# Lo parts of 17 mLSTM weight tiles on VectorE, and the order of loads, sums and splits in three later stages

## The chip, the cores and the metric

One core of a Trainium2 chip runs the kernel in one launch. The metric is device time in microseconds (us), the median of several runs. In the profile PE is TensorE, DVE VectorE, ACT ScalarE, POOL GpSimd and SP SyncE, which here only issues DMAs.

## The reference, cut to what matters

One layer of a diffusion backbone over 1024 latent tokens with 256 context tokens as a prefix, width 1024, all in float32.

```python
def layer(x, c, ctx, c_ctx):
    h = modulate(x, ...)                 # adaLN-modulated RMSNorm, also of ctx
    k, v, ig, fg, q, o, cu, cb, cc, gates = split(h @ w_in)
    conv = ...                           # width-3 convolution along grid rows, gated
    hs = mlstm_chunked(q, k, v, ig, log_sigmoid(fg), state of ctx)   # 8 heads, 2 directions
    merged = sigmoid(gates_a) * (conv @ w_a) + sigmoid(gates_b) * (norm(hs) * sigmoid(o) @ w_b)
    x = x + gate1 * (merged @ w_out)
    h2 = modulate(x, ...)
    return x + gate2 * (square(relu(h2 @ w_f1)) @ w_f2)              # width 4096
```

The output is this latent stream after a last RMSNorm, 1024 x 1024.

## The kernel before, in words

All matrices are multiplied in three passes: a float32 operand is split into `hi`, its value rounded to fp32r, and `lo`, the rest, also in fp32r, and the product is hi·hi + hi·lo + lo·hi (`PASS`). The helper `split` (line 127) makes both parts: `hi` by a copy on ScalarE, `lo` by a subtraction on the engine that its argument `eng_lo` names, or on GpSimd where none is given. Nearly every instruction of the profile carries line 75, the line of a small wrapper that calls the engine; operations are told apart by the names of their tiles. Loads are issued on SP (line 94, `dma`), stores on POOL (line 91, `store`).

The work goes through these stages (us of the span): adaLN and norms to about 100; the mLSTM with its projections to about 517; Strassen products of weight pairs ("H pairs") to about 900; two further GEMMs in 56 steps (`gsteps`) to 1053; the output projection to 1160; Strassen pairs of the MLP's first matrix ("F pairs") to 1450; the MLP's second matrix to 1772.

**Weight tiles.** In the mLSTM stage and in the output projection, tiles of 128 x 1024 are taken from a list, `stream`, of (source, engine of the lo part). `fetch(n)` (line 144) loads and splits tiles until `n` stand ready, `take()` takes one; their pool `ws` has two buffers for each of `wst`, `whi`, `wlo`. For each head pair 1 to 3 the list (line 349) has two V tiles, a K and a Q tile; then come eight O tiles (line 350). Only the second V tile names VectorE. While a tile's matmuls run, a generator `mlstm` (line 572) is pumped for pieces of the mLSTM chunks: on VectorE `e` (decay exponents), `cs` (states), `sdt` (scores times decay), `dn` and `rcp` (the denominator) and `hs` (the output); on GpSimd `wqz` (weighted q); on TensorE `psm`, `pso`, `psu`. The order of these pieces on each engine is found by a scheduler from the dependencies and from the time that it holds each instruction to take; stages with `pinned[0]` set, the H pairs, `gsteps` and F pairs among them, keep the order in which they are written.

**Pairs.** The class `Pairs` (line 831) multiplies two rows of weights, `a` and `c`, by seven products `m1` to `m7` instead of eight. `steady(p0)` (line 942) runs a pair's products while it prepares the next pair's factors: `first_row` splits `a`, `second_block` a half of `c`, `sums` (line 870) makes four sums in place on VectorE, `sums_row` splits them into `sh` (ScalarE) and `sl` (VectorE), and `load_pair` loads the rows of the pair after it. `early` is the first pair that runs in this steady form: 1 for the H pairs, 3 for the F pairs. In that pair `sums` comes after `m5`, in later ones after `m2`. `load_row` (line 845) issues its load unpinned, so that the scheduler places it among SP's other loads.

**MLP pairs.** `f11`, `f22`, `f12`, `f21` finish the four results of a pair, in tiles `fc` and `fd` (in the profile `Ffc` and `Ffd` from the home buffers), with relu and square on ScalarE. `fpost` (line 1467) sums them for the second matrix's own Strassen form and stores them to `fq` in DRAM; its two results `Ff12` and `Ff34` have one home page each, but for pair 1, which takes two pages `f` of the pool `pg` (37 pages).

**The output projection.** Its eight `w_o` tiles (line 1305) have VectorE as lo engine. `fetch(1)` at the third-last of the `gsteps` (line 1328) loads and splits the first one; the others follow as `take` is called. In the same stretch VectorE finishes the merge (`gate`, `u4` and `Ml`, the lo part of the merged operand).

Of the kernel before, what the change touches and what calls it, by code (L numbers as in the profile page):

```python
# [13 lines left out]
P = 128  # L14
# [5 lines left out]
H = 8  # L20
# [19 lines left out]
U_K, U_Q, U_O, U_X, U_GC, U_GB, U_MA, U_MB = 0, 4, 8, 16, 24, 32, 40, 48  # L40
# [20 lines left out]
def tile_block(ctx: ExitStack, tc: tile.TileContext, x, cx, w_mod1, w_mod, w_v0, w_v, w_unit, w_conv, w_mls, w_o, w_f1, w_f2, cols_d, rows_d, cst_d, out):  # L61
    nc = tc.nc
    pinned = [False]
# [18 lines left out]
    V, A, G, PE, SY = Engine(nc.vector), Engine(nc.scalar), Engine(nc.gpsimd), Engine(nc.tensor), nc.sync  # L82
# [10 lines left out]
    def dma(dst, src, pin=True):  # L93
        i = SY.dma_start(dst, src)
        if pin:
            tc.keep_in_program_order(i)
# [3 lines left out]
    def nm(s):  # L100
        uid[0] += 1
        return f"{s}_{uid[0]}"

    def page(shape, dt=F32, name="pg"):
        return pg.tile(shape, dt, tag="pg", name=nm(name))
# [27 lines left out]
    def load_w_now(src, eng_lo=None, eng_hi=None):  # L133
        n = 1024
        st = ws.tile([P, n], F32, tag="wst", name=nm("wst"))
        dma(st, src, pin=False)
        hi = ws.tile([P, n], F32R, tag="whi", name=nm("whi"))
        lo = ws.tile([P, n], F32R, tag="wlo", name=nm("wlo"))
        split(st, hi, lo, eng_hi, eng_lo)
        return hi, lo  # L140

    stream, ready = [], []

    def fetch(n=1):
        while stream and len(ready) < n:
            ready.append(load_w_now(*stream.pop(0)))
# [26 lines left out]
    def keep(f):  # L173


        def call(*a, **kw):
            p, pinned[0] = pinned[0], True
            f(*a, **kw)
            pinned[0] = p

        return call
# [164 lines left out]


    for p in range(1, 4):
        stream += [(w_v[p - 1, :, 0:1024],), (w_v[p - 1, :, 1024:2048], V), (w_unit[U_K + p],), (w_unit[U_Q + p],)]
    stream += [(w_unit[U_O + h],) for h in range(H)] + [(w_unit[U_MB + 4 * i],) for i in range(2)]  # L350


    gb = wm.tile([P, 32], F32, name="gb", bufs=1)
# [449 lines left out]
    def home(n_, i, n, make, dt=F32, shape=(P, 1024)):  # L803

        if (n_, i % n) not in homes:
            homes[n_, i % n] = make(list(shape), dt, n_)
        return homes[n_, i % n]

    def leave(pre):

        for k in [k for k in homes if k[0].startswith(pre)]:
            del homes[k]

    def in_ws(shape, dt, name):
        return ws.tile(shape, dt, tag=name, name=nm(name))
# [7 lines left out]
    def add(o, a, b):  # L823
        V.tensor_tensor(o, a, b, op=ALU.add)
# [6 lines left out]
    class Pairs:  # L831
# [13 lines left out]
        def load_row(self, p, i, own=False):  # L845
            if p >= self.early:
                st = self.home("wst" if p % 2 else "wst2", i, 2, (lambda s_, d_, n_: in_ws(s_, d_, "wst")) if p % 2 else page)
            else:
                st = page([P, 1024], name="wst") if own else in_ws([P, 1024], F32, "wst")
            dma(st, self.rows(p)[i], pin=False)  # L850
            self.raw.setdefault(p, []).append(st)

        def load_pair(self, p):
# [88 lines left out]
        def steady(self, p0, last=None, each=lambda p: None):  # L942
            for p in range(p0, self.n):
                n = p + 1 if p + 1 < self.n else None
                if p > self.early:
                    self.end_d(p - 1)
                self.m1(p)
                if p == self.early:
                    self.end_d(p - 1)
                self.post(p - 1)  # L950
                self.m6(p)
                each(p)
                if n:
                    self.first_row(n)
                    self.second_block(n)
                    if n + 1 < self.n:
                        self.load_pair(n + 1)
                self.m2(p)
                if n and p > self.early:
                    self.sums(n)  # L960
                if n is None and last:
                    last()
                self.m7(p)
                each(p)
                self.m5(p)
                if p == self.early:
                    self.sums(n)
                if n:
                    self.sums_row(n, 0)
                self.m3(p)  # L970
                each(p)
                if n:
                    self.sums_row(n, 1)
                self.m4(p)
# [244 lines left out]
    def each(p):  # L1219
        if p > HE and HPAIRS[p][0] != U_GB:  # L1220
            pump_one()
        if p == len(HPAIRS) - 2:
            drain()
# [6 lines left out]
    gsteps = [(g, m, k) for g in range(2) for m in ORDER7 for k in range(4)]  # L1230
# [32 lines left out]
    def g_prepare(i):  # L1263
        hi, lo = ring("whi", i, F32R), ring("wlo", i, F32R)
        for src, s in zip(gst.pop(i), (L, R)):
            split(src, hi[:, s], lo[:, s], eng_lo=V)
        gmade[i] = hi, lo
# [33 lines left out]
    def block(n_, j, pool=page):  # L1301
        return home(n_, j // 2, 2, pool, F32, (P, 2, 512))[:, j % 2, :]
# [4 lines left out]
    for i, (g, m, k) in enumerate(gsteps):  # L1307
        if i + AHEAD + 1 < len(gsteps):
            g_gather(i + AHEAD + 1)
        if i + AHEAD < len(gsteps):  # L1310
            g_prepare(i + AHEAD)
        X = sets[(g + ORDER7.index(m)) % 2]
        ab = gmade.pop(i)
        for j in range(4):
            for n_, (a, b) in enumerate(PASS):
                keep(PE.matmul)(X[j], ab[a][:, j * P : (j + 1) * P], ab[b][:, R], start=m not in (2, 4) and k == 0 and n_ == 0, stop=k == 3 and n_ == 2, skip_group_check=True)
        if m == 1:
            for n in range(2 * k, 2 * k + 2):
                gate[g, n] = page([P, D], name="gate")
                dma(gate[g, n], sgd[gemms[g][2]][n])  # L1320
                if g == 0:
                    t2[n] = gate[g, n]
        for _ in range(-(-len(later) // (4 - k))):
            later.pop(0)()
        if i == 16:
            hpost(len(HPAIRS) - 1)
            leave("H")
        if i == len(gsteps) - 3:
            fetch(1)
        if k < 3:  # L1330
            continue
        U2, V22 = [[block(n_, j, page2) for j in range(4)] for n_ in ("Gu2", "Gv")]
        for j in range(4):
            if m == 1:
                A.copy(U2[j], X[j])
            elif m == 6:
                later.append(lambda j=j, X=X: add(U2[j], X[j], U2[j]))
            elif m == 2:
                later += gated(g, j, L, lambda j=j, X=X, g=g: mul(gate[g, j][:, L], X[j], gate[g, j][:, L]))
            elif m == 7:  # L1340
                later.append(lambda j=j, X=X: add(V22[j], X[j], U2[j]))
            elif m == 5:
                U4 = [half("u4") for _ in range(4)] if j == 0 else U4
                later.append(lambda j=j, X=X, U4=U4: add(U4[j], X[j], U2[j]))
                later.append(lambda j=j, X=X: add(V22[j], X[j], V22[j]))
            elif m == 4:
                later.append(lambda j=j, X=X: add(U2[j], X[j], U2[j]))
            elif m == 3:
                later.append(lambda j=j, X=X, U4=U4: add(U4[j], X[j], U4[j]))
        if m == 2 and g:  # L1350
            later += [lambda n=n: joined(0, n) for n in range(4)]
        if m == 5:
            for j in range(4):
                later += gated(g, 4 + j, R, lambda j=j, g=g: mul(gate[g, 4 + j][:, R], V22[j], gate[g, 4 + j][:, R]))
        elif m == 4:
            for j in range(4):
                later += gated(g, 4 + j, L, lambda j=j, g=g: mul(gate[g, 4 + j][:, L], U2[j], gate[g, 4 + j][:, L]))
            if g:
                later += [lambda n=n: joined(0, n) for n in range(4, KT)]
        elif m == 3:  # L1360
            for j in range(4):
                later += gated(g, j, R, lambda j=j, g=g, U4=U4: mul(gate[g, j][:, R], U4[j], gate[g, j][:, R]))
# [103 lines left out]

    def fpost(p):
        c, d = fc.pop(p), fd.pop(p)
        g_, h_ = (home("Ff12", 0, 1, page), home("Ff34", 0, 1, in_mst)) if p != 1 else [page([P, 1024], name="f") for _ in range(2)]
        add(g_[:, L], c[:, R], d[:, R])  # L1470
        sub(g_[:, R], g_[:, L], c[:, L])
        store(fq[2][p], g_)
        sub(h_[:, L], c[:, L], c[:, R])
        sub(h_[:, R], d[:, L], g_[:, R])
        store(fq[3][p], h_)
# [267 lines left out]
    for j in range(4):  # L1743
        t = 4 + j
        cuts = (0, 512) if j < 3 else (0, CUT, 512)
        n = len(cuts)
# [118 lines left out]
```

## Time and profile before

| | |
|---|---|
| median of 3 runs | 1806.89 us (1806.43 to 1807.1) |
| the profiled execution: its time, its span | 1808.16 us, 1806.3 us |
| granted TensorE clock, mean | 0.989 |
| busy: PE, PEld | 1749.0 us (97%), 1443.5 us (80%) |
| busy: DVE, ACT, POOL | 1266.3 us (70%), 753.3 us (42%), 230.6 us (13%) |
| on the chain that ended last: PE, DVE, ACT | 69%, 3%, 2% |

The busy share is an average over stages; what bounds one of them is seen in its own stretch. Engines read and write in the order of their queues, so an instruction that waits holds up all that stand behind it on the same engine. In a timeline row the bracket at the end is the time that the engine stood idle before it and what ended that. [...]

### The profile page before, as it was taken

How to read it: one execution, taken by the hardware profiler on the slowest of the kernel's cores; microseconds unless marked ns; L12 is line 12 of the kernel's file. 1: busy time of each engine (PE TensorE's matmuls, PEld its weight loads, DVE VectorE, ACT ScalarE, POOL GpSimd, SP SyncE). 2: the span in 40 equal slices, each digit the busy share in tenths (PEclk: the TensorE clock that was granted, in tenths of full speed). 3: DMA queues.
4: the chain of work that ended last, by engine and by line, in shares of the span. 5: the costliest groups of instructions: out<-in, count | busy, mean ns of one | idle time of the engine just before them, and what ended most of it. 6: DMA issues, size and time to landing. Idle time of an engine off the chain costs nothing.

```text
span 1806.3 us, 23536 instructions
## 1 busy us (share of the span) xinstructions
PE 1749.0 (97%) x8633; PEld 1443.5 (80%) x8633; DVE 1266.3 (70%) x2207; ACT 753.3 (42%) x1237; POOL 230.6 (13%) x286
## 2 busy tenths in 40 slices
PE   6999999999999999999999999999999999999994
PEld 3898889877877888888888878877888888888884
DVE  5557564546685768879789996876666656577785
ACT  5633534456333331222244434644434444344334
POOL 3213222234320000000000001101101100000001
PEclk9999999999999999999999999999999999999997
DMA  8213141412424453534458255225434376666352
GB/s 321 76 51 84 46 91 34 85 53 77 174 95 173 164 175 99 164 122 135 172 183 297 88 187 187 82 96 190 163 129 153 143 256 195 231 224 204 104 186 93
DMA packets 102107, 261.10 MB, mean 145 GB/s; under 512 B 11624, under 2 KB 24808, under 8 KB 101992
## 3 DMA queue, kind: packets, MB, share of 16 engines
q1 hardware_dynamic: 85672, 200.88, 35.0%
q0 software_dynamic: 16320, 58.73, 8.2%
q8 instruction: 67, 1.10, 0.3%
q14 instruction: 48, 0.39, 0.1%
HBM read 198.62 MB, written 60.95 MB: 144 GB/s over the span
## 4 chain that ended last, share of the span: by engine, by line
PE 69%; DVE 3%; ACT 2%; issue 1%; DMA 0%; POOL 0%; ACTq 0%; DVEq 0%; POOLq 0%
PE psg L75 69%; ACT y L75 1%; DVE gate L75 0%; DMA fq<-Ffd 0%; ACT Fsh L75 0%; DVE wlo L75 0%; DVE y L75 0%; ACT fc L75 0%; DVE wst L75 0%; DVE fc L75 0%; DVE x L75 0%; DVE ftmp L75 0%; DVE Ff L75 0%; DVE Fsl L75 0%; DVE ol L75 0%
## 5 line engine op out<-in xcount | busy, mean ns | idle before, releaser
L75 ACT ACTIVATE whi<-wst 128x512 fp32r<-128x512 f32 (+1 forms) x238 | 195.9, 826 | 262.9 <-PE psg L75 164.8
L75 DVE TENSOR_TENSOR wlo<-wst,whi 128x512 fp32r<-128x512 f32 (+1 forms) x219 | 202.3, 927 | 123.4 <-ACT whi L75 121.6
L75 PE MATMUL psg<-whi,wlo 128*128 128x512 f32 (+2 forms) x688 | 266.5, 387 | 0.0
L75 PE MATMUL psg<-whi 128*128 128x512 f32 (+2 forms) x688 | 266.5, 387 | 0.0
L75 PE MATMUL psg<-wlo,whi 128*128 128x512 f32 (+2 forms) x688 | 266.1, 387 | 0.1
L75 PE MATMUL psg<-hh,whi 128*128 128x512 f32 x440 | 177.5, 409 | 0.7 <-ACT u L75 0.7
L75 PE MATMUL psg<-hh,wlo 128*128 128x512 f32 x440 | 173.5, 400 | 1.3 <-DVE wlo L75 1.3
L75 PE MATMUL psg<-hl,whi 128*128 128x512 f32 x440 | 173.0, 399 | 0.0
L75 PEld LDWEIGHTS psg<-wlo,whi 128*128 128x128 f32 x688 | 129.5, 188 | 27.8 <-DVE wlo L75 0.6
L75 PEld LDWEIGHTS psg<-whi,wlo 128*128 128x128 f32 x688 | 129.3, 188 | 27.2
L75 PEld LDWEIGHTS psg<-whi 128*128 128x128 f32 x688 | 129.4, 188 | 26.8
L75 PEld LDWEIGHTS psg<-hh,wlo 128*128 128x128 f32 x440 | 83.9, 191 | 20.7 <-DVE wlo L75 1.7
L75 PEld LDWEIGHTS psg<-hh,whi 128*128 128x128 f32 x440 | 83.3, 191 | 19.7 <-ACT u L75 1.1
L75 PEld LDWEIGHTS psg<-hl,whi 128*128 128x128 f32 x440 | 84.0, 191 | 17.6
L75 PE MATMUL psg<-oh,Fsl 128*128 128x512 f32 x240 | 94.9, 396 | 0.1
L75 PE MATMUL psg<-oh,Fsh 128*128 128x512 f32 x240 | 94.9, 396 | 0.0
L75 PE MATMUL psg<-ol,Fsh 128*128 128x512 f32 x240 | 94.6, 394 | 0.0
L75 DVE TENSOR_TENSOR u<-psg,u 128x512 f32<-128x512 f32 x67 | 45.8, 686 | 50.2 <-PE psg L75 48.5
L75 PE MATMUL psg<-whi,hh 128*128 128x256 f32 (+1 forms) x256 | 76.2, 297 | 0.0
L75 PE MATMUL psg<-whi,hl 128*128 128x256 f32 (+1 forms) x256 | 73.3, 286 | 0.0
L75 PE MATMUL psg<-wlo,hh 128*128 128x256 f32 (+1 forms) x256 | 73.2, 286 | 0.0
L75 POOL TENSOR_TENSOR wqz<-w,q 64x256 f32<-64x256 f32 x64 | 46.9, 735 | 140.4 <-PE pso L75 125.6
(352 smaller groups left out, 3936.6 us busy)
## 6 DMA issues: line engine op xcount, KB each, us to landing
wst<-fq SPq DMA_DIRECT2D x112, 256.0 KB, 2.8
wst<-in_w_unit_dram SPq DMA_DIRECT2D x38, 512.0 KB, 3.8
mst<-in_w_mod_dram SPq DMA_DIRECT2D x32, 512.0 KB, 4.1
wst<-in_w_f_dram SPq DMA_DIRECT2D x64, 256.0 KB, 3.0
fq<-Ff POOLq DMA_DIRECT2D x30, 512.0 KB, 3.1
wst<-in_w_f_dram SPq DMA_DIRECT2D x21, 512.0 KB, 3.5
Hwst<-in_w_unit_dram SPq DMA_DIRECT2D x18, 512.0 KB, 3.5
x<-in_x_dram SPq DMA_DIRECT2D x16, 512.0 KB, 4.7
```

Source lines behind the costliest of these rows:

```text
L75: i = f(*a, **kw)
```

## The change

Five edits. (1) The 15 entries of `stream` without an engine among the V, K, Q and O tiles get `V`, VectorE, as engine of the lo part; with three V tiles, three K, three Q and eight O tiles these are 17. (2) `load_row` pins its load where the code around it is pinned, so that the H and F pairs' loads go out in the order in which they are written. (3) In the first steady pair `sums` comes after `m2`, as in the others. (4) The last three `gsteps` fetch one `w_o` tile each, instead of the third-last alone. (5) Pair 1 of the MLP uses the home pages for its two results instead of two pages of its own.

```diff
     for p in range(1, 4):
-        stream += [(w_v[p - 1, :, 0:1024],), (w_v[p - 1, :, 1024:2048], V), (w_unit[U_K + p],), (w_unit[U_Q + p],)]
-    stream += [(w_unit[U_O + h],) for h in range(H)] + [(w_unit[U_MB + 4 * i],) for i in range(2)]
+        stream += [(w_v[p - 1, :, 0:1024], V), (w_v[p - 1, :, 1024:2048], V), (w_unit[U_K + p], V), (w_unit[U_Q + p], V)]
+    stream += [(w_unit[U_O + h], V) for h in range(H)] + [(w_unit[U_MB + 4 * i],) for i in range(2)]
...
-            dma(st, self.rows(p)[i], pin=False)
+            dma(st, self.rows(p)[i], pin=pinned[0])
...
                 self.m2(p)
-                if n and p > self.early:
+                if n:
                     self.sums(n)
...
                 self.m5(p)
-                if p == self.early:
-                    self.sums(n)
...
-        if i == len(gsteps) - 3:
-            fetch(1)
+        if i >= len(gsteps) - 3:
+            fetch(i - len(gsteps) + 4)
...
-        g_, h_ = (home("Ff12", 0, 1, page), home("Ff34", 0, 1, in_mst)) if p != 1 else [page([P, 1024], name="f") for _ in range(2)]
+        g_, h_ = home("Ff12", 0, 1, page), home("Ff34", 0, 1, in_mst)
```

What this does to the order of instructions is seen in three places, all on VectorE. The first is the mLSTM stage at head pair 2's K and Q tiles. Before (`hs_2498` is the output that TensorE waited for at 251 us):

```order
L75 TENSOR_TENSOR sdt_2748<-psm_519_2746,e_2680 128x256
L75 TENSOR_TENSOR sdt_2752<-psm_521_2750,e_2680 128x256
L75 SCALAR_TENSOR_TENSOR e_2754<-e_2754,gt_a,cst_67 128x128 x4
L75 SCALAR_TENSOR_TENSOR dn_2775<-pso_2741,dn_2775 128x2
L75 TENSOR_TENSOR va_2194<-psg_2723,vb_2191 128x2x128
L75 RECIPROCAL rcp_2778<-dn_2775 128x2
L75 SCALAR_TENSOR_TENSOR hs_2498<-pso_2741,rcp_2778,hs_2498 128x128
```

The same place with the change:

```order
L75 TENSOR_TENSOR sdt_2752<-psm_521_2750,e_2680 128x256
L75 SCALAR_TENSOR_TENSOR e_2754<-e_2754,gt_a,cst_67 128x128 x4
L75 SCALAR_TENSOR_TENSOR dn_2766<-pso_2736,dn_2766 128x2
L75 TENSOR_TENSOR dn_2775<-pso_2741,gt_gd 128x2
L75 RECIPROCAL rcp_2769<-dn_2766 128x2
L75 TENSOR_TENSOR va_2194<-psg_2723,vb_2191 128x2x128
L75 SCALAR_TENSOR_TENSOR dn_2775<-pso_2741,dn_2775 128x2
L75 TENSOR_TENSOR wlo_2800<-wst_2797,whi_2799 128x1024
L75 SCALAR_TENSOR_TENSOR hs_2497<-pso_2736,rcp_2769,hs_2497 128x128
L75 RECIPROCAL rcp_2778<-dn_2775 128x2
L75 TENSOR_TENSOR sdt_2824<-psm_539_2822,e_2754 128x256
L75 SCALAR_TENSOR_TENSOR hs_2498<-pso_2741,rcp_2778,hs_2498 128x128
```

The Q tile's lo part now stands between the `e` group and `hs_2498`, the K tile's one row ahead of the first `sdt`, and the operations of the other direction (`dn_2766`, `rcp_2769`, `hs_2497`), which stood ahead of the `e` group, stand behind it.

The second place is the output projection: `wlo_8956` before, and `wlo_8903` with the change, is the lo part of its third weight tile. Before:

```order
L75 TENSOR_TENSOR u_1159_8727<-psg_5423,u_1159_8727 128x512
L75 TENSOR_TENSOR gate_8324<-u_1156_8724,gate_8324 128x512
L75 TENSOR_TENSOR gate_8326<-u_1157_8725,gate_8326 128x512
L75 TENSOR_TENSOR gate_7751<-gate_7751,gate_8324 128x512
L75 TENSOR_TENSOR gate_7753<-gate_7753,gate_8326 128x512
L75 TENSOR_TENSOR gate_8350<-u_1158_8726,gate_8350 128x512
L75 TENSOR_TENSOR gate_8352<-u_1159_8727,gate_8352 128x512
L75 TENSOR_TENSOR gate_7776<-gate_7776,gate_8350 128x512
L75 TENSOR_TENSOR gate_7778<-gate_7778,gate_8352 128x512
L75 TENSOR_TENSOR wlo_8956<-wst_8953,whi_8955 128x1024
```

With the change:

```order
L75 TENSOR_TENSOR wlo_8873<-wst_8870,whi_8872 128x1024
L75 TENSOR_TENSOR Ml_8889<-gate_7800,Mh_8888 128x512
L75 TENSOR_TENSOR Ml_8889<-gate_7802,Mh_8888 128x512
L75 TENSOR_TENSOR Ml_8895<-gate_7824,Mh_8894 128x512
L75 TENSOR_TENSOR Ml_8895<-gate_7826,Mh_8894 128x512
L75 TENSOR_TENSOR wlo_8903<-wst_8900,whi_8902 128x1024
L75 TENSOR_TENSOR gate_8324<-u_1156_8724,gate_8324 128x512
L75 TENSOR_TENSOR gate_8326<-u_1157_8725,gate_8326 128x512
```

The third tile's lo part has moved from behind the eight `gate` operations to ahead of them; the second tile's, `wlo_8873`, now stands right ahead of the four `Ml`.

The third place is the first steady pair of the MLP, pair 3 (`Fwst` are pair 4's rows, whose sums are made in place). Before:

```order
L75 TENSOR_TENSOR Fa_1346_9966<-Fwst_1357_10131,Fa_1346_9966 128x512
L75 TENSOR_TENSOR Ffc_10204<-psg_5426,u_1358_10159 128x512
L75 TENSOR_TENSOR Ffd_10091<-psg_5425,Ffc_10204 128x512
L75 TENSOR_TENSOR Fwst_1356_10129<-Fwst_1356_10129,Fwst_1357_10131 128x512
L75 TENSOR_TENSOR Fwst_1357_10131<-Fwst_1357_10131 128x512
L75 TENSOR_TENSOR Fwst_1357_10131<-Fwst_1357_10131,Fwst_1356_10129 128x512
L75 TENSOR_TENSOR Fwst_1356_10129<-Fwst_1356_10129,Fwst_1357_10131 128x512
L75 TENSOR_TENSOR Fsl_9404<-Fwst_1357_10131,Fsh_9403 128x1024
```

With the change:

```order
L75 TENSOR_TENSOR Fa_1346_9966<-Fwst_1355_10129,Fa_1346_9966 128x512
L75 TENSOR_TENSOR Fwst_1354_10127<-Fwst_1354_10127,Fwst_1355_10129 128x512
L75 TENSOR_TENSOR Fwst_1355_10129<-Fwst_1355_10129 128x512
L75 TENSOR_TENSOR Fwst_1355_10129<-Fwst_1355_10129,Fwst_1354_10127 128x512
L75 TENSOR_TENSOR Fwst_1354_10127<-Fwst_1354_10127,Fwst_1355_10129 128x512
L75 TENSOR_TENSOR Ffc_10202<-psg_5426,u_1356_10157 128x512
L75 TENSOR_TENSOR Ffd_10091<-psg_5425,Ffc_10202 128x512
L75 TENSOR_TENSOR Fsl_9404<-Fwst_1355_10129,Fsh_9403 128x1024
```

The four sums have moved ahead of `Ffc` and `Ffd`. On SP, pair 4's two rows now go into pages that `fc` of pair 0 and `fd` had, and each pair's two rows are issued one after the other, `a` first.

## Rows read from the trace of the kernel before

**Rows 1.** The page, busy time by engine: us, share, instructions.
```profile
PE 1749.0 (97%) x8633; PEld 1443.5 (80%) x8633; DVE 1266.3 (70%) x2207; ACT 753.3 (42%) x1237; POOL 230.6 (13%) x286
```

**Rows 2.** TensorE's waits: us in total, times, longest.
```profile
PE pso L75 <- DVE hs L75: 7.2, 6, 2.6
PE psg L75 <- ACT u L75: 5.5, 3, 3.7
```

**Rows 3.** TensorE's timeline, rows with a wait: start, us, instruction, [idle before].
```profile
251.31 0.80 PE L75 MATMUL pso<-va,sdt 128*128 128x129 f32 x2 [2.57 <-DVE hs L75]
...
338.07 0.49 PE L75 MATMUL pso<-va,sdt 128*128 128x129 f32 x2 [2.62 <-DVE hs L75]
...
400.51 0.63 PE L75 MATMUL pso<-va,sdt 128*128 128x129 f32 x2 [2.11 <-DVE sdt L75]
...
565.83 0.51 PE L75 MATMUL psg<-hh,whi 128*128 128x512 f32 x1 [0.66 <-ACT u L75]
...
1068.76 0.50 PE L75 MATMUL psg<-wlo,Mh 128*128 128x512 f32 x1 [1.66 <-DVE wlo L75]
...
1243.45 0.50 PE L75 MATMUL psg<-oh,whi 128*128 128x512 f32 x1 [3.69 <-ACT u L75]
```

**Rows 4.** VectorE's timeline, 238 to 250 us.
```profile
239.86 1.13 DVE L75 SCALAR_TENSOR_TENSOR e<-e,gt_a,cst 128x128 f32<-128x128 f32 x4
...
245.12 4.83 DVE L75 SCALAR_TENSOR_TENSOR e<-e,gt_a,cst 128x128 f32<-128x128 f32 x4
```

**Rows 5.** VectorE's timeline at 332 us.
```profile
331.84 4.88 DVE L75 SCALAR_TENSOR_TENSOR e<-e,gt_a,cst 128x128 f32<-128x128 f32 x4
```

**Rows 6.** GpSimd's timeline, 125 to 517 us.
```profile
243.45 2.37 POOL L75 TENSOR_TENSOR wlo<-wst,whi 128x1024 fp32r<-128x1024 f32 x1 [3.40 <-ACT whi L75]
...
247.46 2.34 POOL L75 TENSOR_TENSOR wlo<-wst,whi 128x1024 fp32r<-128x1024 f32 x1
...
390.60 2.38 POOL L75 TENSOR_TENSOR wlo<-wst,whi 128x1024 fp32r<-128x1024 f32 x1 [2.65 <-ACT whi L75]
```

**Rows 7.** VectorE's timeline, 388 to 401 us.
```profile
388.66 0.61 DVE L75 SCALAR_TENSOR_TENSOR cs<-cs,md,us 64x129 f32<-64x129 f32 x2 [0.43 <-ACT us L75]
...
390.81 2.59 DVE L75 SCALAR_TENSOR_TENSOR cs<-cs,md,us 64x129 f32<-64x129 f32 x2 [0.63 <-ACT us L75]
```

**Rows 8.** Stretches: length, busy PE, PEld, DVE, ACT, POOL, granted clock, DMA, GB/s.
```profile
226.00:271.00 45.00, 42.43 (x288) 38.01 (x287) 27.86 (x106) 16.79 (x52) 13.46 (x14) 0.92 0.47 91
316.00:361.00 45.00, 42.38 (x292) 38.04 (x291) 26.78 (x101) 19.78 (x58) 12.31 (x14) 0.96 0.41 85
361.00:406.00 45.00, 42.89 (x222) 34.56 (x222) 21.20 (x62) 24.94 (x44) 16.62 (x18) 0.96 0.18 53
1039.00:1084.00 45.00, 42.91 (x188) 34.45 (x188) 42.35 (x63) 16.42 (x24) 3.44 (x2) 1.00 0.52 188
...
1240.00:1264.00 24.00, 20.55 (x82) 16.63 (x83) 13.46 (x20) 10.60 (x13) 2.14 (x4) 0.93 0.40 142
```

**Rows 9.** VectorE's timeline at 289 us, a V tile's lo part.
```profile
289.13 1.23 DVE L75 TENSOR_TENSOR wlo<-wst,whi 128x1024 fp32r<-128x1024 f32 x1 [14.06 <-ACT whi L75]
```

**Rows 10.** VectorE's timeline, 1053 to 1077 us, the first two of eight.
```profile
1062.67 1.28 DVE L75 TENSOR_TENSOR gate<-u,gate 128x512 f32<-128x512 f32 x2
```

**Rows 11.** VectorE's timeline, 1214 to 1246 us.
```profile
1224.35 0.69 DVE L75 TENSOR_TENSOR Ff<-fc 128x512 f32<-128x512 f32 x1
...
1230.42 0.69 DVE L75 TENSOR_TENSOR Ffd<-psg,Ffc 128x512 f32<-128x512 f32 x1 [1.60 <-DMA fq<-Ffd]
...
1232.47 1.42 DVE L75 TENSOR_TENSOR Fwst<-Fwst,Fwst 128x512 f32<-128x512 f32 x2
1234.35 1.23 DVE L75 TENSOR_TENSOR Fsl<-Fwst,Fsh 128x1024 fp32r<-128x1024 f32 x1 [0.46 <-ACT Fsh L75]
```

**Rows 12.** Pair 1's two stores of `f`, issued 1217.9 and 1219.1: least, median, longest.
```profile
DMA to landing us min/median/max: 4.1/7.2/10.3
```

**Rows 13.** VectorE's timeline, 546 to 568 us, first steady H pair.
```profile
554.05 0.69 DVE L75 TENSOR_TENSOR Hx<-psg,u 128x512 f32<-128x512 f32 x1 [5.71 <-PE psg L75]
```

## The prediction

> **What bounds the kernel now.** I read the page first: TensorE is busy for 1749.0 of 1806.3 us, and no other engine passes 70% [rows 1]. The matrix work stays as it is, so the change can only give back time in which TensorE stands idle or runs slowly, or add such time. So the second view is the list of TensorE's waits; its longest entries after the start are `pso` on VectorE's `hs`, 7.2 us in six waits, and `psg` on ScalarE's `u`, 5.5 us in three [rows 2]. GpSimd isn't waited for anywhere in that list; how can it help to take work from it? That is the third step, the timelines around the long waits.
>
> At 251.31 and 338.07 TensorE had stood still for 2.57 and 2.62 us for `hs`, at 400.51 for 2.11 us for `sdt` [rows 3]. Ahead of that `hs` on VectorE stand four `e` operations, which took 4.83 us in the one case and 4.88 in the other; the same four took 1.13 us at 239.86 [rows 4, 5]. What differs is GpSimd: `wlo` tiles of 2.37 and 2.34 us ran from 243.45 and 247.46, and the `e` group ended at 249.95, just after the second of them (249.80) [rows 4, 6]. Ahead of the `sdt` two `cs` took 2.59 us, under the tile of 390.60, against 0.61 for two of them at 388.66 [rows 6, 7]. So here an operation of VectorE that reads SBUF alone stands until GpSimd's tensor operation is over.
>
> The long waits cost twice. [...] The other long waits are one on a weight tile (1.66 us at 1068.76) and one on `u` in the MLP pairs (3.69 us at 1243.45, in a stretch of 24 us at 0.93, so 1.7 us lost again) [rows 3, 8].
>
> **The change, part by part.**
>
> *Edit 1, 17 lo tiles.* A tile takes GpSimd 2.37 us and VectorE 1.23 [rows 6, 9]; VectorE gets 17 x 1.23 = 20.9 us more work and loses the stalls. By place:
> - Pair 2's K and Q: the four `e` return 4.83 - 1.13 = 3.70 us; two tiles, 2.46, now stand ahead of the awaited `hs`. 1.2 us are left, and the gap of 2.57 shrinks to 1.3. After the 1.66 at 1068.76 the stretch shows full clock [rows 3, 8], so I take the slow stretch as gone: 1.2 + 3.6 = 4.8.
> - Pair 3's K and Q, the same: 4.88 - 1.13 - 2.46 = 1.3, plus 1.8: 3.1.
> - The third O tile: 2.59 - 0.61 - 1.23 = 0.7 of the gap of 2.11, plus 1.8: 2.5 (bounds: nothing, and all of 2.11 and 1.8, 3.9).
> - Pair 1's K and Q: the four other waits on `hs` have 7.2 - 2.57 - 2.62 = 2.0 us together [rows 2, 3], so 2.0 at most is to be had; 2.46 could be added. I take 0, since at pair 2 the return outweighed the tiles.
> - The fourth and fifth O tile: no long wait there, so up to 1.23 each could come ahead of `hs`. Bounds 0 and 2.5; I take 1.2 lost, the middle, as no row is nearer to one end.
> - The V tiles and the other O tiles: the row shown for a V tile has VectorE idle for 14.06 us before it [rows 9]; such waits hide 1.23 us. Without that cover each would cost up to 1.23.
>
> Together 4.8 + 3.1 + 2.5 - 1.2 = 9.2 us.
>
> *Edit 4, three `w_o` tiles early.* The third tile's lo part waits behind a run of eight `gate` operations from 1062.67, 0.6 us each, and TensorE waits 1.66 us for it [rows 3, 10]. Now it stands ahead of those eight, 8 x 0.6 = 4.8 us sooner, so that wait goes. The same work still precedes the fourth tile, which keeps its place. The two extra loads queue on SP ahead of `x1`, which is wanted later. Gain 1.7; bounds 0 (the fourth tile is waited for instead) and 1.7.
>
> *Edits 2, 3 and 5, the MLP pairs.* VectorE reached `Ffd` at 1228.82 and waited there 1.60 us for a store; the four sums, 0.7 us each, stand behind it, and from them the chain runs over `Fsh` and `Fsl` (1234.35) to `u` and TensorE's 3.69 us [rows 3, 11]. With the sums ahead, 2.8 us of them run from about 1228.1, `Ffc` and `Ffd` (0.7 us each) follow, and the latter ends at 1232.3; then the first `Fsl` can start, instead of at 1234.35. The chain is 2.0 us shorter, the gap 1.7, and with the slow stretch of 1.7 gone the gain is 3.7. The sums need pair 4's rows early; their pages are now those of `fc` and `fd` that come free sooner. In written order a pair's second page is loaded up to 4 us later; it is wanted a pair later, and the slowest transfer that I found there took 10.3 [rows 12]: nothing, unless it meets the stores.
>
> *Edits 2 and 3 in the first Strassen pairs.* VectorE waits 5.71 us before 554.05 and then does the sums [rows 13]; moved into that wait, they are off the way to the `u` for which TensorE waited 0.66 us at 565.83 [rows 3]: 0.7 (bounds 0 and 0.7).
>
> **Sum.** 9.2 + 1.7 + 3.7 + 0.7 = 15.3 us. The profiled execution took 1808.16 us (span 1806.3); the median of the runs shown is 1806.89. For such an execution the forecast is 1792.9; a difference carries over, so for the median it is 1806.89 - 15.3 = 1791.6.
>
> **Rivals.**
> *The clock falls all the same.* Of the 15.3 us, 3.6 + 1.8 + 1.8 + 1.7 = 8.9 are slow stretches that I let vanish since gaps of 1.3 to 1.7 remain. If they stay, the time is 1800.5. Against it: full clock around the gap of 1.66. For it: a gap of only 2.11 was followed by one, so the point is near. Chance 0.15. [...]
>
> *The store takes over.* A pair's `Ff` results now lie in one home page for pair 1 too. Pair 2 writes it at 1224.35, while pair 1's store from it, issued at 1219.1, took 10.3 us, to 1229.4 [rows 11, 12]. If it lands as late as that, VectorE stands 5.0 us with everything behind it; the wait of 1.60 disappears in that, and the sums' 2.0 remains, so `u` comes 1.4 us later than before and the slow stretch stays: 1806.9 - 11.6 + 1.4 = 1796.7. For it: the 10.3; against it: pair 4's loads go out earlier, so less is in flight with that store. It decides from a landing after 1227. Chance 0.13.
>
> *VectorE's queue becomes the bound: slower.* If the four `e` were slow for another reason than GpSimd's tiles, nothing is returned, while two tiles, 2.46 us, enter the chain at three K and Q places and one of 1.23 at three O tiles: 11.1 us. Pair 1's gap, 2.0 at most, grows beyond 2.5 and gets a slow stretch of 1.8. Less the 6.1 of the other parts, that is 6.8 slower: 1813.7. It decides from four `e` that take over 1.13 + 1.2 = 2.3 us with GpSimd at rest. For it: VectorE's chain is what TensorE waits for in this stage; against it: the end of the `e` group with the tile's, to 0.15 us. Chance 0.07.
>
> *VectorE holds up GpSimd.* `wqz`, which stays on GpSimd, may stand behind a tile on VectorE; at six K and Q tiles that is 6 x 1.23 = 7.4 lost: 1799.0. Against it: before, GpSimd's own tile of 2.37 us stood in that place [rows 6]. Chance 0.03. [...]
>
> **How the numbers follow.** The likeliest case has 0.58; 0.04 is left for gains that cancel. About 0.2%, 3.6 us, can be told from no change; the first, second and fourth rival lie beyond that on the fast side, less some 0.06 for losses that add to them. Faster 0.58 + 0.15 + 0.13 + 0.03 - 0.06 = 0.83; the same 0.04 + 0.05 = 0.09; slower 0.07 + 0.01 = 0.08. If the gaps that I leave (1.3, 1.3, 1.4, 1.7) closed as well, 5.7 us more would go, and with the 1.2 at the O tiles the time is 1784.7. The range is 1784.5 to 1805: its top takes in the rivals at 1796 to 1801 and some loss beside them, not the slow one.
>
> **What would show it.** No `wlo` on GpSimd in the mLSTM stage; the four `e` near 1.13 us; no wait of `pso` on `hs` or `sdt` above 1.7 us; granted clock 1.00 from 226 to 406; no wait of 1.66 us in the output projection; the wait for `u` in the MLP pairs below 2 us. I am wrong if `hs` or `sdt` waits stay above 2 us with GpSimd at rest, or if an `Ff` operation waits microseconds for a store.

## The result and the profile after

The changed kernel takes 1784.74 us (median of 4, 1784.53 to 1785.03) against 1806.99 of the kernel before (1806.43 to 1808.44 in the same comparison). The ratio is 0.9876 with a 95% interval of 0.9859 to 0.9893, so 22.3 us or 1.2% faster. The forecast of 1791.6 had the direction right, and the places but for one (head pair 1 of the mLSTM stage, which it put at nothing); the size was too small, and the time lies at the lower edge of the stated range. The profiled execution took 1784.66 us, its span is 1782.9.

The page's busy line, which answers to [rows 1]: GpSimd lost 38 us, VectorE gained only 3, though 17 tiles of 1.22 us went over to it. (The first hunk of the diff names VectorE for 17 entries of the list, not for 15 as the text above it has it.)

```profile
PE 1738.9 (98%) x8633; PEld 1433.6 (80%) x8633; DVE 1269.6 (71%) x2224; ACT 754.8 (42%) x1239; POOL 192.8 (11%) x269
```

TensorE's waits, which answer to [rows 2]: total, times, longest. `hs` has gone from 7.2 us to 0.9, `u` from 5.5 to 1.5; a wait for `Ffd` has grown to 1.5.

```profile
PE psg L75 <- ACT u L75: 1.5, 2, 1.2
PE psg L75 <- DVE Ffd L75: 1.5, 2, 1.2
PE pso L75 <- DVE hs L75: 0.9, 3, 0.5
```

The same work now lies 9 to 22 us earlier, so the stretches that answer to [rows 8] start earlier too. Three of mLSTM work and one of the MLP pairs (length, busy PE, PEld, DVE, ACT, POOL, granted clock, DMA, GB/s) all show a granted clock of 1.00, and TensorE busy for 44.6 to 44.8 of 45 us in the mLSTM stage where it was 42.4 to 42.9:

```profile
217.00:262.00 45.00, 44.79 (x336) 40.30 (x335) 33.34 (x126) 18.79 (x55) 9.73 (x12) 1.00 0.38 91
300.00:345.00 45.00, 44.80 (x330) 40.04 (x329) 32.59 (x124) 18.39 (x59) 9.74 (x12) 1.00 0.39 89
345.00:390.00 45.00, 44.56 (x246) 36.14 (x246) 22.59 (x64) 26.98 (x49) 10.34 (x15) 1.00 0.18 51
1218.00:1242.00 24.00, 23.66 (x103) 18.81 (x102) 14.95 (x22) 11.98 (x15) 2.67 (x5) 1.00 0.44 156
```

Where the time came from is read from TensorE's timeline, by the start of the same instruction before and after. The first row (the start of the H pairs) stood at 536.79 before, with a wait of 1.39; the second (the first tile of the output projection) at 1055.66, also with a wait of 0.43; the third is the row at 1243.45 of [rows 3].

```profile
520.09 0.47 PE L75 MATMUL psg<-oh,a 128*128 128x512 f32 x1 [1.40 <-DVE Ha L75]
...
1038.08 0.50 PE L75 MATMUL psg<-wlo,Mh 128*128 128x512 f32 x1 [0.43 <-DVE wlo L75]
...
1221.60 0.50 PE L75 MATMUL psg<-oh,whi 128*128 128x512 f32 x1 [0.34 <-ACT u L75]
```

So 16.7 us are gained up to the H pairs, 0.9 in them (17.6 at the output projection), and 21.9 by the MLP's `u`; with the slow stretch after it, which is gone, the span is 23.4 us shorter. Of the 16.7 us 0.4 are no effect of the change: they are there at 46 us already, before the first tile that moves, after a shorter wait for the very first weights (11.21 us instead of 11.73).

VectorE's timeline at pair 2's K and Q tiles shows the stage's new state, beside [rows 4]. The two tiles stand in the queue as the order said, the four `e` take 1.61 us instead of 4.83, and the `hs` that was late comes at 246.49. The 0.5 us over the undisturbed 1.13 stand beside a `wqz`, a multiplication that stays on GpSimd and runs from 240.65 for 2.39 us (shown near the end):

```profile
240.30 1.22 DVE L75 TENSOR_TENSOR wlo<-wst,whi 128x1024 fp32r<-128x1024 f32 x1
241.44 0.75 DVE L75 TENSOR_TENSOR sdt<-psm,e 128x256 f32<-128x256 f32 x2
242.10 1.61 DVE L75 SCALAR_TENSOR_TENSOR e<-e,gt_a,cst 128x128 f32<-128x128 f32 x4
...
244.29 1.22 DVE L75 TENSOR_TENSOR wlo<-wst,whi 128x1024 fp32r<-128x1024 f32 x1
...
246.49 0.35 DVE L75 SCALAR_TENSOR_TENSOR hs<-pso,rcp,hs 128x128 f32<-128x128 f32 x1 [0.33 <-ACT hs L75]
```

Over all 128 `e` of the stage (us 125 to 505), before and after, the least, median and longest of one, in ns: the median is the same, the long ones are gone.

```profile
L75 DVE SCALAR_TENSOR_TENSOR e<-e,gt_a,cst x128: 333/346/2492, 142.9 to 433.9; 128x128 f32<-128x128 f32 x128
L75 DVE SCALAR_TENSOR_TENSOR e<-e,gt_a,cst x128: 336/346/890, 141.9 to 418.3; 128x128 f32<-128x128 f32 x128
```

In the output projection the third tile's lo part runs at 1045.09, ahead of the `gate` operations, and TensorE has no wait there; beside [rows 10]:

```profile
1045.09 1.22 DVE L75 TENSOR_TENSOR wlo<-wst,whi 128x1024 fp32r<-128x1024 f32 x1
1046.23 1.29 DVE L75 TENSOR_TENSOR gate<-u,gate 128x512 f32<-128x512 f32 x2
```

And in the MLP pairs the sums fill VectorE's time, with no wait for the store; beside [rows 11]. `Ff` at 1204.86 doesn't wait for pair 1's store either; that store, issued at 1199.56, took 4.3 us instead of 10.3:

```profile
1204.86 0.69 DVE L75 TENSOR_TENSOR Ff<-fc 128x512 f32<-128x512 f32 x1
...
1209.84 1.42 DVE L75 TENSOR_TENSOR Fwst<-Fwst,Fwst 128x512 f32<-128x512 f32 x2
...
1211.90 0.69 DVE L75 TENSOR_TENSOR Ffd<-psg,Ffc 128x512 f32<-128x512 f32 x1
1212.51 1.22 DVE L75 TENSOR_TENSOR Fsl<-Fwst,Fsh 128x1024 fp32r<-128x1024 f32 x1
```

### The profile page after: what moved, and what is told of

Same layout as the page of the kernel before. It is cut to its first block, busy times and chain, and to the rows that moved or that the text cites. A ratio compares the mean times of both kernels' runs of the same rounds, so it can differ in the third digit from the quotient of the medians.

```text
span 1782.9 us, 23518 instructions
## 1 busy us (share of the span) xinstructions
PE 1738.9 (98%) x8633; PEld 1433.6 (80%) x8633; DVE 1269.6 (71%) x2224; ACT 754.8 (42%) x1239; POOL 192.8 (11%) x269
## 4 chain that ended last, share of the span: by engine, by line
PE 65%; DVE 4%; ACT 2%; issue 1%; ACTq 0%; DVEq 0%
PE psg L75 65%; ACT y L75 1%; DVE wlo L75 1%; DVE gate L75 0%; DVE wst L75 0%; ACT Fsh L75 0%; DVE y L75 0%; ACT fc L75 0%; DVE fc L75 0%; DVE Gv L75 0%; DVE x L75 0%; DVE ftmp L75 0%; DVE Ff L75 0%; DVE Fsl L75 0%; DVE u L75 0%
## 5 line engine op out<-in xcount | busy, mean ns | idle before, releaser
L75 DVE TENSOR_TENSOR wlo<-wst,whi 128x512 fp32r<-128x512 f32 (+1 forms) x236 | 223.5, 950 | 144.5 <-ACT whi L75 144.0
```

Of the source, the lines that this page charges most:

```text
L75: i = f(*a, **kw)
```

## The experiments

The mLSTM stage gave 16.7 us where the forecast had 9.2. The theory was that this comes from edit 1 alone, because VectorE stands while GpSimd runs a tensor operation on SBUF; the rivals were that the new order, the sooner lo parts or the later edits have a share, and that VectorE's queue has its price. Medians of the kernel before were 1806.9, 1807.15 and 1806.05 us in the three groups of runs; differences from the changed kernel's 1784.74 go across groups, so that one of about 1 us is taken only where a trace shows it too.

**Edit 1 alone, and all without it.** The kernel before with the first hunk of the diff; and the changed kernel with that hunk undone.

> Edit 1 alone, the 17 lo parts on VectorE. In the changed kernel the stages up to the start of the H pairs are 16.4 us shorter than before, the later ones 6.7. Theory (each stage's gain belongs to the edits made in it): about 1790.5 us, 16.4 less than before, with TensorE's waits on hs below 1 us and no slow stretch from 226 to 406. Rival (a part of the mLSTM gain needs the later edits, or a part of the later gain comes from this one): outside 1789.5 to 1791.5.

> Edits 2 to 5 without edit 1. Theory: 1800.3 us, 6.7 less than before: 0.9 in the H pairs, 1.9 in the output projection, 3.9 in the MLP pairs; the waits of 2.57, 2.62 and 2.11 us and their slow stretches stay. Rival (the parts overlap): less than 5 or more than 8 below before.

Measured: 1790.6 us with edit 1 alone (1788.89 to 1792.48), 16.3 below before; 1800.96 without it (1798.32 to 1802.51), 5.9 below. Together 22.2, the whole result: within the spread of these runs, some 2 us to either side, the parts are independent. Edit 1 alone brings the start of the H pairs to 520.02 us, as in the changed kernel. It keeps the later waits of before: TensorE waits 1.68 us on the third `w_o` tile and 3.19 on `u` in the MLP pairs.

**GpSimd does the subtractions as well, for nothing.** In the changed kernel, for the 17 tiles:

```diff
         split(st, hi, lo, eng_hi, eng_lo)
+        if extra:
+            G.tensor_tensor(st, st, hi.bitcast(F32), op=ALU.subtract)
```

> The changed kernel, but GpSimd does the 17 subtractions as well, afterwards and for nothing, into the staging tile that is then free. The order on TensorE, VectorE and ScalarE stays that of the changed kernel but for a few rows. Theory (VectorE stands while GpSimd runs a tensor operation on SBUF): the four e operations take over 3 us again at several K and Q tiles, waits above 2 us and slow stretches return, and the time goes up by 8 to 18 us, to 1793 to 1803. Rival (the gain is that the lo parts are ready sooner, or the new order of the pieces): within 2 us of 1784.7, since both stay.

Measured: 1805.7 us (1800.44 to 1807.48 over ten runs), 21 above the changed kernel and within 0.3% of before; more than the theory's 8 to 18. At the K and Q tiles VectorE's order is the new one, the lo parts are VectorE's own, and still nearly all is lost. VectorE's and then GpSimd's timeline at pair 2's K and Q:

```profile
247.54 3.82 DVE L75 SCALAR_TENSOR_TENSOR e<-e,gt_a,cst 128x128 f32<-128x128 f32 x4
```

```profile
246.09 2.40 POOL L75 TENSOR_TENSOR wqz<-w,q 64x256 f32<-64x256 f32 x2 [3.63 <-PE pso L75]
248.56 2.40 POOL L75 TENSOR_TENSOR wst<-wst,whi 128x1024 f32<-128x1024 f32 x1
```

The `e` group ends at 251.36, one `e` of 0.35 us after GpSimd's subtraction at 250.96. TensorE's waits on `hs` and `sdt` are back, and with them stretches of low clock:

```profile
PE pso L75 <- DVE hs L75: 7.0, 5, 1.9
PE psg L75 <- DVE wlo L75: 4.2, 3, 2.5
PE pso L75 <- DVE sdt L75: 3.0, 2, 2.6
```

```profile
231.00:276.00 45.00, 43.11 (x298) 38.34 (x297) 29.64 (x105) 20.08 (x60) 14.08 (x14) 0.96 0.45 90
388.00:433.00 45.00, 42.06 (x222) 33.84 (x220) 33.45 (x104) 24.76 (x49) 14.01 (x14) 0.92 0.34 83
```

Not all of the 21 us is VectorE's standing. The `wlo` that TensorE waited 2.5 us for ran at 487.71, behind two `Hsl`; in the changed kernel it runs at 462.20, ahead of them. So that wait, and the 1.7 us of the slow stretch after it, come from an order that differs there. Taken off, some 17 us are left for it, within the theory's 8 to 18.

**GpSimd fills instead of subtracting.** The same place, with a write in place of the subtraction:

```diff
+        if extra:
+            for _ in range(2):
+                G.memset(st, 0.0)
```

> The changed kernel, with GpSimd filling each of the 17 staging tiles with zeros twice after its last use: GpSimd is as busy there, but reads nothing from SBUF. If any tensor operation of GpSimd makes VectorE stand, e operations are long again and the time goes up as far as these fills last, by 3 us or more. [...]

Measured: 1784.14 us (1783.88 to 1784.43), not slower than the changed kernel. GpSimd was at work at the very place, from 243.35 and 245.81 for 1.96 us each, and VectorE's tile at 244.54 took 1.22 us beside it, as it does alone. At 379.55 eight `e` ran beside two other fills in 2.18 us, 0.27 us from one to the next. Of all the `e` in this run 21 ran beside fills alone, and none took over 0.35 us.

```profile
243.35 1.96 POOL L75 MEMSET wst<- 128x1024 f32 x2
245.81 1.96 POOL L75 MEMSET wst<- 128x1024 f32 x2 [0.50 <-DVE wlo L75]
...
379.09 1.96 POOL L75 MEMSET wst<- 128x1024 f32 x2 [3.85 <-DVE wlo L75]
```

```profile
244.54 1.22 DVE L75 TENSOR_TENSOR wlo<-wst,whi 128x1024 fp32r<-128x1024 f32 x1
...
379.55 2.18 DVE L75 SCALAR_TENSOR_TENSOR e<-e,gt_a,cst 128x128 f32<-128x128 f32 x8
```

So in these runs it isn't GpSimd's being busy, nor its writing, that stops VectorE; what the subtraction has and the fill has not is the reading of SBUF. `e`, with two inputs in SBUF, stands beside subtractions (up to 2.55 us for one) and not beside fills (0.35 at most). The trace of the kernel before shows which operations of VectorE are spared: 20 `hs` and 38 `sdt`, which take one input from PSUM, ran beside GpSimd's tensor operations, and none took over 0.35 and 0.43 us.

**The kernel before, with fills for the lo parts.** GpSimd fills the 17 lo tiles with zeros; the lo parts of these weights are left out.

```diff
+        if eng_lo is None and n_lo[0] < 17:
+            n_lo[0] += 1
+            A.activation(hi, st, AF.Copy)
+            for _ in range(2):
+                G.memset(lo.bitcast(F32), 0.0)
+        else:
             split(st, hi, lo, eng_hi, eng_lo)
```

> The kernel before, but GpSimd fills the 17 lo tiles with zeros (twice, some 2 us a tile) instead of computing them, so the lo parts of 17 weights are left out. GpSimd is nearly as busy as before and reads nothing from SBUF there; VectorE gets no tile; the order on TensorE, ScalarE and, but for a few rows, VectorE is that of before. Theory (GpSimd's reading alone makes the mLSTM stage slow, and neither the new order nor VectorE's faster subtraction is needed): the four e operations fall to about 1.13 us, the waits of 2.57, 2.62 and 2.11 us fall below 0.6, and the time is 1788 to 1792, like edit 1 alone. Rival (the new order on TensorE gives a good part): waits over 1 us stay, 1795 to 1803.

Measured: 1793.67 us (1791.27 to 1794.17), 12.4 below before, a little above the theory's range. With the old order and no tile on VectorE the H pairs start at 522.43 us: 14.4 earlier than before, where edit 1 has 16.7. TensorE's waits on `hs` are at 0.8 in all. So the end of VectorE's stalls beside GpSimd's subtractions is worth about 14 us without the new order. One thing comes with the fills: they don't wait for `hi`, so they are over sooner than the subtractions were (240.08 against 243.45 at pair 2's K tile). That has little to give, since before no wait of TensorE ended on GpSimd's `wlo`. What the other 2.3 us are due to, this run doesn't show; the new order of TensorE is one candidate. After the wait on `u` in its MLP pairs the granted clock of 24 us is 0.86, where it was 0.93 [rows 8]; that takes 1.7 us of the gain back in the profiled execution, as it does with edit 1 alone.

```profile
PE pso L75 <- DVE hs L75: 0.8, 2, 0.5
```

**VectorE does the subtractions twice.**

```diff
+        if extra:
+            V.tensor_tensor(st, st, hi.bitcast(F32), op=ALU.subtract)
```

> The changed kernel, but VectorE does each of the 17 subtractions twice, the second time for nothing: 17 x 1.23 = 20.9 us more work in VectorE's queue. My working took a tile's 1.23 us as lengthening the chain wherever it stands ahead of an hs (2.46 at each K and Q pair, 1.23 at O tiles): by that the gaps of 0.2 to 0.5 grow by as much, 8 to 12 us in all and more if slow stretches come, 1793 to 1800. Rival (VectorE has room in this stage once GpSimd is quiet, and its idle time takes in the tiles): below 1788.

Measured: 1789.05 us (1788.63 to 1789.15), 4.3 above the changed kernel: between the two expectations, and nearer to the rival's. Of 20.9 us more work in VectorE's queue a fifth shows. The scheduler knows of this work too and moved instructions on TensorE and VectorE for it, so the 4.3 us are the price with that help. TensorE's waits:

```profile
PE psg L75 <- DVE wlo L75: 3.7, 4, 1.8
PE pso L75 <- DVE hs L75: 3.4, 7, 0.8
```

**Parts of the MLP change.** The changed kernel with one of the edits 3, 5 and 2 undone.

> The changed kernel with edit 3 undone: the sums of the first steady pair stand after m5 again, the loads and pages stay new. Theory (both edits relieve the wait: the store of Ffd already lands in time, and the sums only stand 1.2 to 1.4 us in the way): the wait for u in the MLP pairs grows from 0.34 to about 1.6 us without a slow stretch, and 0.9 us of the H pairs go: 1786.8. Rival (the sums carry all of it): the wait of 3.7 us and the slow stretch come back: 1789.5.

> The changed kernel with edit 5 undone: pair 1 of the MLP has its two own pages again, so pair 4's rows take other, later pages. Theory (the sums carry the gain): the wait on u stays below 1 us, the time within 1 us of 1784.7. Rival (the earlier pages and less crowded stores carry it): VectorE waits for the store of Ffd or ScalarE for pair 4's rows, 1.5 to 3.7 us slower, 1786.2 to 1788.4.

> The changed kernel with edit 2 undone: the pairs' loads go out where the scheduler puts them. Theory (loads have room in both stages): within 1 us of 1784.7. Rival (the written order keeps loads and stores apart): over 1 us slower, with a wait on a store or on rows of weights in the MLP pairs.

Without edit 3: 1788.09 us (1787.89 to 1789.59), 3.4 above, between the theory's 1786.8 and the rival's 1789.5. The row shows why. The chain to `u` is short, as the theory had it, but TensorE comes to it about 1.1 us sooner since it doesn't wait 1.24 us for `Ffd` ahead of it; so the gap is 2.68 us, and a slow stretch follows (0.93 over 24 us, 1.7 us lost):

```profile
1223.25 0.50 PE L75 MATMUL psg<-oh,whi 128*128 128x512 f32 x1 [2.68 <-ACT u L75]
```

```profile
1220.00:1244.00 24.00, 21.32 (x86) 16.87 (x85) 13.45 (x19) 10.78 (x13) 2.14 (x5) 0.93 0.39 146
```

Without edit 5: 1785.98 us (1785.49 to 1786.82), 1.2 above and a little past the theory's 1 us; the trace shows 1.1 of it. Pair 4's rows are loaded later, at 1198.80 instead of 1188.07, among the stores, and the store of `Ffd` takes 9.1 us to landing where it takes 4.8 in the changed kernel. VectorE waits for it again, and TensorE for `Ffd`, 2.4 us instead of 1.2:

```profile
1213.00 0.69 DVE L75 TENSOR_TENSOR Ffd<-psg,Ffc 128x512 f32<-128x512 f32 x1 [1.15 <-DMA fq<-Ffd]
```

Without edit 2: 1784.64 us (1784.26 to 1785.0), no difference. The written order of the loads gives nothing by itself.

**The same at the start.** In the first 45 us, too, VectorE stands under GpSimd's subtractions (of modulation weights): in the changed kernel a tile at 35.11 takes 3.42 us, and TensorE waits 1.27 us for it.

```profile
34.91 9.27 POOL L75 TENSOR_TENSOR wlo<-wmod,whi 128x1024 fp32r<-128x1024 f32 x3 [4.35 <-ACT whi L75]
```

```profile
35.11 3.42 DVE L75 TENSOR_TENSOR wlo<-wst,whi 128x1024 fp32r<-128x1024 f32 x1
```

The changed kernel with the five tiles on VectorE as well (`LO_G = ()`), and with three of them (`LO_G = (6, 9)`):

> The changed kernel, with the five modulation tiles' lo parts at the start (20 to 45 us) on VectorE as well. There a subtraction of VectorE takes 3.42 us and a small operation 2.14 us under three tiles of GpSimd, and TensorE waits 1.27 us at 37.3 us. Theory: the same exclusion is at work; VectorE gets 6.1 us more and loses some 5 us of stalls, and the wait falls to 0.3: 1 to 2.5 us faster, 1782.3 to 1783.7. Rival (VectorE is the bound at the start and the five tiles enter its queue): 1 to 4 us slower.

> As the run before, but the first two of the five tiles (21 to 28 us) stay on GpSimd, where no long operation of VectorE stands beside them. Theory: 0 to 1 us faster than with all five moved. Rival (VectorE is the bound at the start): slower than the changed kernel, by less than with all five.

Measured: 1786.25 us with five (1785.46 to 1787.13), 1.5 above the changed kernel; 1788.75 with three (1785.76 to 1791.65), two runs near 1786 and two near 1791.5, so no clear value but not better. (The mean granted clock was 0.991 in the latter two, one of them the profiled one, and 0.993 and 0.995 in the other two.) Both theories about a gain fell. VectorE's and GpSimd's timelines with five tiles:

```profile
34.44 1.22 DVE L75 TENSOR_TENSOR wlo<-wmod,whi 128x1024 fp32r<-128x1024 f32 x1 [0.28 <-ACT whi L75]
...
36.19 2.30 DVE L75 TENSOR_TENSOR wlo<-wst,whi 128x1024 fp32r<-128x1024 f32 x1
```

```profile
35.81 1.60 POOL L75 TENSOR_TENSOR hl<-mtmp,hh 128x512 fp32r<-128x512 f32 x1 [5.99 <-ACT hh L75]
```

The awaited tile now starts 1.1 us later, behind a moved one, and another GpSimd subtraction, `hl`, runs at that moment and stands in its way: the tile takes 2.30 us instead of 1.22 and ends at 38.49, as before the move (38.53). So nothing is gained there, and at 45.87 TensorE waits 1.44 us for one of three modulation tiles that VectorE now does in a row; at 149.5 us the run is 1.0 us behind the changed kernel.

## Why the prediction was right, and where its size was off

*What bounds, and by what mechanism.* Right. The long waits of the mLSTM stage came from GpSimd's tensor operations, not from VectorE's own work: with GpSimd's subtraction put back the gain is lost (1805.7 us) though VectorE's work stays; with fills it stays (1784.14).

*Edit 1: 9.2 us forecast, 16.3 measured in the medians (16.7 in the profiled execution up to the H pairs).* This is the mis-sized term. The stalls and the slow stretches were read rightly (but see the rivals for the ground on which the latter were taken as gone). The 3.6 and 1.8 us that it counts for slow stretches are 45 us times the 0.08 and 0.04 by which 0.92 and 0.96 fall short of 1.00 [rows 8]; the trace of the kernel before has the granted clock at 0.50 from 251 to 257 us, from 340 to 342 and from 401 to 404, and in the slow stretch of the MLP pairs, from 1244.17 to 1246.73, matmuls of 128x512 start 0.43 us apart, against 0.23 from 1247.43 on. The step that failed is "two tiles, 2.46, now stand ahead of the awaited `hs`. 1.2 us are left, and the gap of 2.57 shrinks to 1.3". The longest waits left at pairs 2 and 3 are 0.2 us each, that at the third O tile is 0.43 instead of the 1.4 left in the forecast, and no loss came at the fourth and fifth O tile. A tile in VectorE's queue is not a tile on the way to TensorE: 17 of them, done twice, cost 4.3 us. One reason is in the trace. Before, TensorE went from the scores, `psm` at 248.25, straight to the `pso` of 251.31. Now the scheduler, which knows of VectorE's work, puts five matmuls of the projection between the two, so that TensorE works while VectorE's chain runs:

```profile
244.53 0.28 PE L75 MATMUL psm<-q,kT 64*128 64x128 f32 x2
244.74 0.50 PE L75 MATMUL psg<-hh,whi 128*128 128x512 f32 x1
245.08 0.39 PE L75 MATMUL psg<-hl,whi 128*128 128x512 f32 x1
245.31 0.39 PE L75 MATMUL psg<-hh,wlo 128*128 128x512 f32 x1
245.54 0.39 PE L75 MATMUL psg<-hh,whi 128*128 128x512 f32 x1
245.77 0.39 PE L75 MATMUL psg<-hl,whi 128*128 128x512 f32 x1
246.00 0.38 PE L75 MATMUL pso<-va,sdt 128*128 128x129 f32 x2
```

The forecast looked at VectorE's order at this place and not at TensorE's. The run with fills, where the stalls end and no tile enters VectorE's queue, has 14.4 us, so taking the tiles off was the error: with them edit 1 gained no less. Pair 1, which I had at 0, gave 1.2 us: its waits of 1.05 and 0.17 on `hs` at 161 and 163 us are gone.

That the range's lower sum, 1784.7 with all gaps closed, is the measured time is luck in part: 0.8 us of the gaps at pairs 2 and 3 and the third O tile and 1.0 of new waiting for `Ffd` remain, and pair 1, which that sum has at nothing, makes up for some of it.

*Edit 4: 1.7 us.* Right: the wait of 1.66 us is gone, the first tile's 0.43 stayed, the fourth is not waited for. From the output projection's first tile to TensorE's wait in the MLP, 1055.66 to 1243.45 before and 1038.08 to 1221.60 after, 4.3 us were gained; 1.7 of them are this wait.

*Edits 2, 3 and 5, the MLP: 3.7 us.* Right in sum: 2.4 us of waiting and 1.7 of the slow stretch, 4.1. The wait on `u` fell by 3.35 us, further than the 2.0 of the shorter chain, since TensorE now waits 1.24 us for `Ffd` earlier; 3.69 + 0.28 became 0.34 + 1.24, and the slow stretch went. The parts are now known: undoing edit 3 costs 3.4 us, here and in the H pairs together; undoing edit 5 costs 1.2, by the store; edit 2 nothing. That the pages for pair 4's rows matter by way of a store's landing was named in the forecast, but no price was put on it.

*The H pairs: 0.7 us.* Measured 0.9, with the sums in VectorE's idle time; without edit 3 the wait is back, 0.68 us at 549.07.

*The rivals.* The clock did not fall in the mLSTM stage and the MLP, where the gaps came out far smaller than I had left them, so that rival was not put to the test by the change. The ground against it, full clock around a gap of 1.66, was weak: in the same trace the clock fell after the wait of 1.26 us at 38.95 (0.50 from 39 to 42 us), and in the run with GpSimd's second subtraction after 1.87 us at 253.47 (0.96 from 231 to 276). Had the gaps of 1.3 been left, the slow stretches might have stayed. The store did not take over: `Ff` at 1204.86 follows the operation before it directly. VectorE's queue did not become the bound in the stages that were changed. GpSimd is held up in turn, as the fourth rival had it, but TensorE doesn't wait for it: two `wqz` took 2.39 us beside VectorE's tile, against 1.53 five microseconds earlier.

```profile
235.48 1.53 POOL L75 TENSOR_TENSOR wqz<-w,q 64x256 f32<-64x256 f32 x2 [3.89 <-PE pso L75]
240.65 2.39 POOL L75 TENSOR_TENSOR wqz<-w,q 64x256 f32<-64x256 f32 x2 [3.64 <-PE pso L75]
```

## What to carry to other kernels

Where VectorE's short SBUF operations show a mean far above their median (here 459 ns against 346 for `e`), look at what GpSimd reads at that moment: an engine that nobody waits for can still be the one that sets the pace, and here 38 us of it cost about 14. Price work that is moved onto a busy engine by whether its waits hide it, and read the new order of the waiting engine, not only of the one that gets the work; here the full price was five times too high. And moving the reader isn't always a gain: at the start of this kernel, where another subtraction of GpSimd stood beside the awaited tile all the same, the move gained nothing and came out 1.5 us slower.

## What was not expected of the hardware

The length of a gap alone doesn't tell whether the granted clock falls. A wait of 2.11 us on `sdt` was followed by a stretch at 0.96 in the kernel before [rows 3, 8]; the same wait of 2.11 us in the kernel without edit 1 was followed by full clock:

```profile
388.00:433.00 45.00, 42.06 (x241) 33.04 (x240) 36.29 (x114) 27.73 (x57) 16.84 (x17) 1.00 0.29 77
```

After 2.35 us in the kernel without edit 5 the clock stayed full as well (1.00 from 1212 to 1236), while after 3.19 us with edit 1 alone 24 us went at 0.86. Among the shorter ones, the wait of 1.27 us at 38.59 in the changed kernel was followed by 0.50 from 39 to 42 us, and a nearly equal one of 1.24 us at 1212.64 in the same kernel by full clock (1.00 up to 1225). The kernels with long waits also spread more: 1798.3 to 1802.5 us without edit 1 and 1800.4 to 1807.5 with GpSimd's second subtraction, against 1784.5 to 1785.0 for the changed kernel. The mean granted clock, on record for every run, goes with these times. Without edit 1 it was 0.993 in the two runs below 1799 us and 0.990 to 0.992 in the four above 1800; with GpSimd's second subtraction it was 0.993 to 0.994 in the four runs below 1803 and 0.988 to 0.991 in the six above 1805. So stretches of low clock come and go between runs of one kernel; where in the kernel they fell is known for the profiled executions alone.
